# The first mixer of a two-layer trunk: one input block of the recurrent branch ahead of the queries, the other behind, and the gates as a process of their own

## The chip, the core and the metric

The kernel runs on one core of a Trainium2 chip. The metric is the device time of one execution in microseconds (us). Five engines work beside each other: TensorE (PE, with its weight loads PEld), VectorE (DVE), ScalarE (ACT), GpSimd (POOL) and SyncE (SP), which issues most of the transfers. Each engine works through its own row of instructions in order and waits at semaphores for the others.

## The reference

A trunk of two layers over 512 tokens of width 1024, all in float32, with a modulation of every sub-layer by a condition `c`. The first layer is the one that matters here:

```python
def layer_ab(...):
    sh_m, sc_m, g_m, sh_f, sc_f, g_f = adaln(c, mod_w, mod_b)       # silu(c) @ mod_w + mod_b
    h = modulate(x, norm_mix, sh_m, sc_m)                           # rmsnorm(x) * (1 + sc_m) + sh_m
    (a_gate, a_x, q, kc, vc, ks, vs, kw, vw, gts) = _split(h @ w_in, IN0_SIZES)
    y_a = rg_lru(causal_conv(a_x, conv_w, conv_b), wa, ba, wx, bx, lam) * jax.nn.gelu(a_gate)
    y_b = nsa_mixer(q, kc, vc, ks, vs, kw, vw, jax.nn.sigmoid(gts), ...)
    x = x + g_m[:, None, :] * (jnp.concatenate([y_a, y_b], axis=-1) @ w_out)
    h = modulate(x, norm_ffn, sh_f, sc_f)
    return x + g_f[:, None, :] * swiglu(h, wg, wu, wd)

def rg_lru(x, ...):                      # per channel
    r = sigmoid(x_blocks @ wa + ba);  i = sigmoid(x_blocks @ wx + bx)
    log_a = -8 * r * softplus(-lam)
    u = sqrt(-expm1(2 * log_a)) * (i * x)
    h[t] = exp(log_a)[t] * h[t-1] + u[t]
```

`nsa_mixer` has 8 query heads in 2 groups and works on blocks of 128 queries: attention to 31 compressed blocks, to the best 8 of 8 blocks of 64 keys (so to all that the mask allows) and to a window, summed with gates. The second layer is an attention with an indexer, again with a feed-forward; a last norm ends the trunk.

## The kernel before

**Matmuls in three passes.** A weight block of 1024 rows x 256 columns (1 MB) is loaded by SyncE into one of four buffers named `raw` (`load_next`, L163, and L167 for the parts of w_out). `split` rounds it on ScalarE to `whi` (L173) and takes the rest `wlo` on VectorE, or on GpSimd for the second half of some of w_out (L174). `passes` issues three matmuls for each of 8 contraction steps: rounded weight by rounded activation (L387), rounded weight by the rest (L388), rest by rounded activation (L389). `pair` does this for both 128-column halves of a block.

**Order of loads.** The list `entries` is the order in which blocks are loaded and split. In layer 0 it holds the input blocks of w_in ("win" window keys, "gts" gates, "q0" and "q1" queries, "ax0" and "ax1" the recurrent branch, "ag0" and "ag1" its gate branch), then four blocks of w_out. Behind each come some blocks of the modulation weights (`emit_mods`; the numbers per block are `MIX_MODS`), which share the four buffers. A modulation block is multiplied with `silu_c` on TensorE (`mod_rows`, L256, eight instructions) or, by other code, on GpSimd; L267 sums the rows.

**Order of work.** Generator processes yield modelled durations to a `Weaver`, which always advances the one of the lowest priority number that is ready. The first mixer has a process `backbone` (priority 5: window keys, gates, queries, recurrent branch, gate branch, output projection) and attention processes of higher rank, which start as soon as their queries are set. After that a list scheduler sets each engine's row at build time, so the rows of an engine are fixed when the program runs.

**Names.** Queries are evacuated from PSUM by ScalarE (L1009) and VectorE (L1010, `qs`). The recurrent branch: `lru1` is the convolution (ScalarE L863, then three VectorE taps L865, `xc`); `lru_gates` has two block-diagonal matmuls per 128 channels (L873, L875), two tanh on ScalarE (L878, L879) and a product (L880); `lru2` forms the recurrence's factors (ScalarE L889, L890, L897, GpSimd, VectorE L894) and scans (L902). The gate branch is evacuated at L1145. In attention a head's scores are L499, L500 and a mask matmul L510 into `b_sc`; maximum L515, exponential L518, transposes of the weights L534 (copied at L536), the weighted sum L555 into `b_o`; the compressed branch has L1083, L1086, L1111 and L548. The concatenated output is split into `yhi` and `ylo` (L1126 and L1127, L1159 and L1160) and goes through the output projection in two token halves, so its matmuls are 256 columns wide.

Of the kernel before, what the change touches and what calls it, by code (L numbers as in the profile page):

```python
# [19 lines left out]
KT = D // P  # L20
# [77 lines left out]
def trunk(ctx, tc, I, out):  # L98
    nc = tc.nc
    wv = Weaver()  # L100
# [8 lines left out]
    def bank(tag):  # L109
        return ps.tile([P, 512], F32, name="b_" + tag, tag=tag)  # L110
# [32 lines left out]
    def add_w(key, name, r0, nk, c0, ncols, cuts):  # L143
        entries.append(("w", key, name, r0, nk, c0, ncols, cuts))

    def add_mod(layer, part, j, handler):
        entries.append(("m", (layer, part, j), "l%d_mod_w" % layer, 0, KT, part * D + j * 256, 256, handler))
# [29 lines left out]
    def pump(share):  # L177

        jobs = state["jobs"]
        while jobs and state["done"] < share * state["total"]:  # L180
            state["done"] += 1
            jobs.pop(0)()
# [32 lines left out]
    def need(key, spread=False):  # L215

        idx = next(n for n, e in enumerate(entries) if e[0] in "wh" and e[1] == key)
        nxt = next((n for n in range(idx + 1, len(entries)) if entries[n][0] in "wh"), None)
        if nxt is None:
            nxt = idx + sum(e[0] == "f" for e in entries[idx + 1:idx + 3])  # L220
        pump(1.0)
        todo = list(range(state["proc"], nxt + 1))
        state["proc"] = max(state["proc"], nxt + 1)
        todo = [n for n in todo if entries[n][0] != "m"] + [n for n in todo if entries[n][0] == "m"]
        now = [n for n in todo if n <= idx or not spread]
        ms = [n for n in now if entries[n][0] == "m"]
        for i in now:
            if entries[i][0] != "m":
                process(i)
        if ms:  # L230
            wv.spawn(paced(ms), -5)
        jobs = [lambda i=i: process(i) for i in todo if i not in now]
        state["jobs"], state["done"], state["total"] = jobs, 0, len(jobs)
# [149 lines left out]
    def passes(o, w, rhi, rlo, nk, start=True, stop=True):  # L383

        hi, lo = w
        for k in range(nk):
            mm(o, hi[:, k], rhi(k), start=(start and k == 0), stop=False)  # L387
            mm(o, hi[:, k], rlo(k), start=False, stop=False)  # L388
            mm(o, lo[:, k], rhi(k), start=False, stop=(stop and k == nk - 1))  # L389
            yield k  # L390

    def pair(key, nk, ncut, rh, rl, tags, evac, flag=None):

        need(key)
        ws = [units.pop((key, n)) for n in range(ncut)]
        for n in range(ncut):
            o = bank(tags[n])
            m = ws[n][0].shape[-1]
            run = passes(o[:m], ws[n], lambda k: rh(k, 0, S), lambda k: rl(k, 0, S), nk)
            for k in range(nk):  # L400
                if flag is not None and n == 0:
                    yield ("until", flag(k))
                next(run)
                pump((n * nk + k + 1.0) / (ncut * nk))
                yield 3 * MM
            evac(n, o[:m], 0, S)
# [253 lines left out]
    def emit_mods(lst, n):  # L660
        for _ in range(n):
            if lst:
                l, p, j = lst.pop(0)
                entries.append(("m", (l, p, j), "l%d_mod_w" % l, 0, KT, p * D + j * 256, 256, "later"))
# [8 lines left out]
    add_mod(0, 0, 2, None)  # L673
    add_mod(0, 1, 3, None)
    add_mod(0, 0, 3, None)
    for nm, c0 in (("win", 2048), ("gts", 2304), ("q0", 1024), ("q1", 1280), ("ax0", 512), ("ax1", 768), ("ag0", 0),
                   ("ag1", 256)):
        if nm == "gts":
            entries.append(("h", ("in0", nm), W0, 0, KT, c0, 24, None))
        else:  # L680
            add_w(("in0", nm), W0, 0, KT, c0, 256, (P, P))
        emit_mods(dve_mods, MIX_MODS[nm])
# [162 lines left out]
    def layer0():  # L845
        mp = mix_ctx.enter_context(tc.tile_pool(name="mix0", bufs=1))
        rh = lambda k, t0, t1: hhi[:, k, t0:t1]
        rl = lambda k, t0, t1: hlo[:, k, t0:t1]
        T2 = ("mm", "mm")
# [10 lines left out]
        def lru1(ft, o):  # L860

            xc = XC[ft] = mp.tile([P, S], F32, name="xc", tag="xc", bufs=2)
            nc.scalar.activation(xc, o, AF.Identity, scale=cw[:, 12 + ft:13 + ft], bias=col["l0_conv_b"][:, ft:ft + 1])  # L863
            for s in (1, 2, 3):
                nc.vector.scalar_tensor_tensor(xc[:, s:], o[:, :S - s], cw[:, 4 * (3 - s) + ft:4 * (3 - s) + ft + 1],  # L865
                                               xc[:, s:], op0=OP.mult, op1=OP.add)
            wv.set(("xc", ft), LRU_WAIT)
# [15 lines left out]
        def lru2(n):  # L883

            fts = (2 * n, 2 * n + 1)
            yield ("wait", 1500.0)
            for ft in fts:
                AA[ft] = mp.tile([P, S], F32, name="la", tag="lx", bufs=4)
                nc.scalar.activation(AA[ft], R[ft], AF.Exp, scale=k8[:, ft:ft + 1], bias=k8[:, ft:ft + 1])  # L889
                nc.scalar.activation(R[ft], R[ft], AF.Tanh, scale=p8[:, ft:ft + 1], bias=p8[:, ft:ft + 1])  # L890
            for ft in fts:
                a2 = mp.tile([P, S], F32, name="a2", tag="xc", bufs=2)
                nc.gpsimd.tensor_tensor(a2, AA[ft], AA[ft], op=OP.mult)
                nc.vector.scalar_tensor_tensor(R[ft], a2, 1.0, R[ft], op0=OP.add, op1=OP.mult)  # L894
            yield ("wait", 4000.0)
            for ft in fts:
                nc.scalar.activation(R[ft], R[ft], AF.Sqrt, scale=0.25)  # L897
                nc.gpsimd.memset(R[ft][:, 0:1], 0.5)
                nc.gpsimd.tensor_tensor(R[ft], R[ft], IX[ft], op=OP.mult)
            yield ("wait", 2500.0)  # L900
            for ft in fts:
                nc.vector.tensor_tensor_scan(R[ft], AA[ft], R[ft], 0.0, op0=OP.mult, op1=OP.add)  # L902
                yield ("wait", 1200.0)
            wv.set(("lru", n))
# [142 lines left out]
        def kv_evac(br):  # L1047
            def f(n, o, t0, t1):
                if n == 0:
                    dup_k(Ks, br, o, mp, "kk", 2)  # L1050
                else:
                    v_rows(Vs, br, o, mp, "xc", 2)
            return f
# [111 lines left out]
        def backbone():  # L1165
            need(("in0", "win"))
            for n, ev in enumerate((cmp_evac, kv_evac(1))):
                for z in range(2):
                    for k in kv_g[2 * n + z]:
                        yield 3 * MM  # L1170
                    ev(z, kv_o[2 * n + z], 0, S)
            for y in pair(("in0", "win"), KT, 2, rh, rl, ("o", "o"), kv_evac(2)):
                yield y
            wv.set("kv2", CMP_WAIT)
            for y in gts_unit(("in0", "gts")):
                yield y
            for j in range(2):
                def qe(n, o, t0, t1, j=j):
                    sq_(4 * j + 2 * n, o)
                    wv.set(("q", 4 * j + 2 * n), 2000.0)  # L1180
                    wv.set(("q", 4 * j + 2 * n + 1), 2500.0)
                for y in pair(("in0", "q%d" % j), KT, 2, rh, rl, T2, qe):
                    yield y
            for j in range(2):
                for y in pair(("in0", "ax%d" % j), KT, 2, rh, rl, T2, lambda n, o, t0, t1, j=j: lru1(2 * j + n, o)):
                    yield y
                if j:
                    yield ("until", ("lru", 0))
                for ft in (2 * j, 2 * j + 1):
                    yield ("until", ("xc", ft))  # L1190
                    for y in lru_gates(ft):
                        yield y
                wv.spawn(lru2(j), -4)
            yield ("until", ("lru", 1))
            for j in range(2):
                for y in pair(("in0", "ag%d" % j), KT, 2, rh, rl, T2, lambda n, o, t0, t1, j=j: ag_evac(2 * j + n, o)):
                    yield y
            wv.spawn(y_a(), -6)
            for y in out_proj(0, mp):
                yield y  # L1200
            wv.set("mix0")

        wv.spawn(backbone(), 5)
        wv.run()
        mix_ctx.close()
# [411 lines left out]
```

## Time and profile before

| | |
|---|---|
| runs | 1302.85, 1303.10, 1303.66 us (median 1303.1) |
| profiled execution | 1303.04 us |
| its span | 1301.2 us |
| granted TensorE clock, mean | 0.990 |
| TensorE busy | 1257.3 us, 97% |
| VectorE busy | 774.1 us, 59% |
| ScalarE busy | 506.0 us, 39% |
| GpSimd busy | 268.4 us, 21% |
| transfers | 153.52 MB, mean 118 GB/s |

The profiled execution's time is 1.8 us above its span; that part lies around the program. Times on the trace's axis start at the span's start. The first mixer's backbone stands at 88 us (first query evacuation 89.34) to about 310; the gate branch's last evacuation is at 201.74, the first output matmul at 222.89. A line such as `PE b_mm L387 <- ACT whi L173: 1.8, 1, 1.8` reads: TensorE, at line 387 with output `b_mm`, waited for ScalarE's `whi` of line 173, 1.8 us in total, once, 1.8 at the longest.

### The profile page before, as it was taken

The page shows a single profiled execution, that of the slowest core. Times are in us where ns is not written, and L with a number is a line of the kernel's source. Part 1 is how long each engine was busy: PE and PEld are TensorE (multiplying, and loading weights), DVE is VectorE, ACT ScalarE, POOL GpSimd, SP SyncE. Part 2 cuts the span into 40 slices and gives each one's busy share as a digit, 9 for nine tenths or more (in the row PEclk, how much of TensorE's full clock was granted, in tenths as well). Part 3 has the DMA queues.
Part 4 walks back from the last instruction along what each step waited for, and adds up shares of the span by engine and source line. Part 5 has one row for each costly group of instructions (what it writes and reads, how often), then busy time and mean ns, then how long its engine had stood idle before and what let it go on. Part 6 is the DMA issues. An engine that isn't in the chain of part 4 may idle for free.

```text
span 1301.2 us, 17845 instructions
## 1 busy us (share of the span) xinstructions
PE 1257.3 (97%) x7024; PEld 1041.9 (80%) x7024; DVE 774.1 (59%) x1482; ACT 506.0 (39%) x935; POOL 268.4 (21%) x213
## 2 busy tenths in 40 slices
PE   6999998999999999999999997999999999999997
PEld 4777676789888888888898776778988888888886
DVE  6455876758656567656667699954833333333434
ACT  3444765534322222212235545774432222222323
POOL 2310142011225335344423422003000000000003
PEclk9999999999999999999999999999999999999999
DMA  9954123532544555656542523001232332233201
GB/s 325 261 167 142 62 67 98 133 96 98 162 129 162 169 178 172 194 193 195 170 131 65 130 44 86 1 2 45 86 97 97 97 98 97 97 97 97 99 16 65
DMA packets 151651, 153.52 MB, mean 118 GB/s; under 512 B 6632, under 2 KB 149136, under 8 KB 151568
## 3 DMA queue, kind: packets, MB, share of 16 engines
q1 hardware_dynamic: 150560, 151.24, 37.4%
q8 instruction: 55, 0.90, 0.3%
q10 hardware_dynamic: 656, 1.08, 0.2%
q14 instruction: 28, 0.23, 0.1%
q0 software_dynamic: 352, 0.07, 0.0%
HBM read 150.28 MB, written 2.10 MB: 117 GB/s over the span
## 4 chain that ended last, share of the span: by engine, by line
PE 84%; DVE 8%; ACT 3%; SPq 2%; DMA 2%; issue 1%; POOLq 0%; POOL 0%; ACTq 0%; DVEq 0%
PE b_mm L387 12%; PE b_mm L388 12%; PE b_mm L389 12%; PE b_sc L387 10%; PE b_sc L388 10%; PE b_sc L389 10%; PE b_o L555 2%; PE b_tp L534 2%; SPq L163 1%; PE b_sc L499 1%; DVE isc L1502 1%; PE b_sc L500 1%; DMA raw<-in_l_mod_w 1%; PE b_tp L256 1%; DVE m L1501 1%
## 5 line engine op out<-in xcount | busy, mean ns | idle before, releaser
L173 ACT ACTIVATE whi<-raw 128x1024 fp32r<-128x1024 f32 (+1 forms) x175 | 182.5, 1047 | 502.0 <-PE b_mm L388 206.4
L174 DVE TENSOR_TENSOR wlo<-raw,whi 128x1024 fp32r<-128x1024 f32 (+1 forms) x148 | 200.1, 1355 | 137.4 <-ACT whi L173 135.4
L387 PE MATMUL b_mm<-fh,whi 128*128 128x512 f32 x320 | 126.3, 395 | 0.0
L387 PE MATMUL b_sc<-fh,whi 128*128 128x512 f32 x320 | 124.7, 390 | 0.0
L388 PE MATMUL b_mm<-fl,whi 128*128 128x512 f32 x320 | 124.6, 389 | 0.0
L389 PE MATMUL b_sc<-fh,wlo 128*128 128x512 f32 x320 | 124.5, 389 | 0.0
L388 PE MATMUL b_sc<-fl,whi 128*128 128x512 f32 x320 | 124.5, 389 | 0.0
L389 PE MATMUL b_mm<-fh,wlo 128*128 128x512 f32 x320 | 124.4, 390 | 0.0
L285 POOL TENSOR_TENSOR raw<-raw,silu_c 128x1024 f32<-128x1024 f32 x28 | 59.8, 2155 | 229.8 <-DMA raw<-in_l_mod_w 133.1
L174 POOL TENSOR_TENSOR wlo<-raw,whi 128x1024 fp32r<-128x1024 f32 (+1 forms) x27 | 65.2, 2425 | 147.1 <-ACT whi L173 143.2
L1277 DVE TENSOR_TENSOR sg<-sg,b_sc 128x512 f32<-128x512 f32 (+1 forms) x48 | 30.5, 641 | 97.5 <-PE b_sc L389 97.5
L1404 POOL TENSOR_TENSOR xall<-xall,raw 128x512 f32<-128x512 f32 (+1 forms) x9 | 10.5, 1168 | 377.9 <-ACT ftmp L1403 377.9
L387 PE MATMUL b_mm<-hhi,whi 128*128 128x512 f32 x208 | 83.9, 408 | 2.2 <-DVE qs L1010 1.5
L389 PE MATMUL b_mm<-hhi,wlo 128*128 128x512 f32 x208 | 82.7, 398 | 0.0
L388 PE MATMUL b_mm<-hlo,whi 128*128 128x512 f32 x208 | 82.7, 398 | 0.0
L288 POOL TENSOR_TENSOR raw<-raw 128x1024 f32<-128x1024 f32 (+2 forms) x42 | 77.5, 1844 | 3.3
L389 PEld LDWEIGHTS b_mm<-fh,wlo 128*128 128x128 f32 x320 | 60.1, 188 | 13.0
L389 PEld LDWEIGHTS b_sc<-fh,wlo 128*128 128x128 f32 x320 | 60.1, 188 | 12.6
L387 PEld LDWEIGHTS b_sc<-fh,whi 128*128 128x128 f32 x320 | 60.1, 188 | 12.4
L388 PEld LDWEIGHTS b_sc<-fl,whi 128*128 128x128 f32 x320 | 60.1, 188 | 12.4
L388 PEld LDWEIGHTS b_mm<-fl,whi 128*128 128x128 f32 x320 | 60.1, 188 | 12.1
L387 PEld LDWEIGHTS b_mm<-fh,whi 128*128 128x128 f32 x320 | 60.1, 188 | 12.0
(380 smaller groups left out, 2971.4 us busy)
## 6 DMA issues: line engine op xcount, KB each, us to landing
raw<-in_l_mod_w SPq DMA_DIRECT2D x42, 1024.0 KB, 5.3
raw<-in_l_ffn_wg SPq DMA_DIRECT2D x22, 1024.0 KB, 5.4
raw<-in_l_ffn_wu SPq DMA_DIRECT2D x22, 1024.0 KB, 7.4
raw<-in_l_ffn_wd SPq DMA_DIRECT2D x19, 1024.0 KB, 4.9
raw<-in_l_w_in SPq DMA_DIRECT2D x16, 1024.0 KB, 5.5
rawm<-in_l_mod_w SPq DMA_DIRECT2D x6, 1024.0 KB, 11.3
raw<-in_l_w_out SPq DMA_DIRECT2D x12, 512.0 KB, 5.0
raw<-in_l_ffn_wd SPq DMA_DIRECT2D x4, 768.0 KB, 6.7
```

The costliest lines, as they stand in the source:

```text
L163: nc.sync.dma_start(v[:, :k0], I[name][r0:r0 + k0 * P, cs].rearrange("(k p) n -> p k n", p=P))
L173: nc.scalar.activation(hi, raw, AF.Copy)
L174: (eng or nc.vector).tensor_tensor(lo, raw, hi.bitcast(F32), op=OP.subtract)
L256: mm(b[32 * g:32 * g + 32, 0:256], sc_c[:, k:k + 1].to_broadcast([P, 32]), raw[:, k], start=(r == 0), stop=(r == 1), skip_group_check=True)
L285: nc.gpsimd.tensor_tensor(raw[:, k:k + 4], raw[:, k:k + 4], sc_c[:, k:k + 4][:, :, None].to_broadcast([P, 4, 256]), op=OP.mult)
L288: nc.gpsimd.tensor_tensor(raw[:, 0:n], raw[:, 0:n], raw[:, n:2 * n], op=OP.add)
L387: mm(o, hi[:, k], rhi(k), start=(start and k == 0), stop=False)
L388: mm(o, hi[:, k], rlo(k), start=False, stop=False)
L389: mm(o, lo[:, k], rhi(k), start=False, stop=(stop and k == nk - 1))
L534: nc.tensor.transpose(b[:, j * P:(j + 1) * P], pt[:, j * P:(j + 1) * P], ident)
L555: mm(o[64 * z:64 * z + 64, cs].rearrange("p (h q) -> p h q", h=nh), v[:, kb, z * 64:(z + 1) * 64], pT[z][:, :, kb * P:(kb + 1) * P], start ...
L1277: nc.vector.tensor_tensor(t, t, o, op=OP.mult)
```

## The change

The block "ax0" moves ahead of "q0" in `entries`, with the modulation blocks that follow it. `backbone` is cut into `queries(j)`, `recurrent(j)` and `gates(j)`, and its order becomes recurrent 0, queries 0, queries 1, recurrent 1. `gates(j)`, which the backbone went through itself right behind the recurrent block, is spawned as a process of priority 4, one ahead of the backbone.

```diff
-    for nm, c0 in (("win", 2048), ("gts", 2304), ("q0", 1024), ("q1", 1280), ("ax0", 512), ("ax1", 768), ("ag0", 0),
-                   ("ag1", 256)):
+    for nm, c0 in (("win", 2048), ("gts", 2304), ("ax0", 512), ("q0", 1024), ("q1", 1280), ("ax1", 768),
+                   ("ag0", 0), ("ag1", 256)):
...
-            for j in range(2):
-                def qe(n, o, t0, t1, j=j):
+            def queries(j):
+                def qe(n, o, t0, t1):
                     sq_(4 * j + 2 * n, o)
                     wv.set(("q", 4 * j + 2 * n), 2000.0)
                     wv.set(("q", 4 * j + 2 * n + 1), 2500.0)
-                for y in pair(("in0", "q%d" % j), KT, 2, rh, rl, T2, qe):
+                return pair(("in0", "q%d" % j), KT, 2, rh, rl, T2, qe)
+
+            def recurrent(j):
+                for y in pair(("in0", "ax%d" % j), KT, 2, rh, rl, T2, lambda n, o, t0, t1: lru1(2 * j + n, o)):
                     yield y
-            for j in range(2):
-                for y in pair(("in0", "ax%d" % j), KT, 2, rh, rl, T2, lambda n, o, t0, t1, j=j: lru1(2 * j + n, o)):
-                    yield y
+                wv.spawn(gates(j), 4)
+
+            def gates(j):
                 if j:
                     yield ("until", ("lru", 0))
                 for ft in (2 * j, 2 * j + 1):
...
                 wv.spawn(lru2(j), -4)
+
+            for part, j in ((recurrent, 0), (queries, 0), (queries, 1), (recurrent, 1)):
+                for y in part(j):
+                    yield y
             yield ("until", ("lru", 1))
```

The first place is VectorE's row at the start of the backbone; `qs` rows evacuate queries, `xc` rows are taps of the convolution, `mod_` rows sum modulation blocks.

```order
 L174 TENSOR_TENSOR wlo<-raw,whi 128x1024
-L1010 SCALAR_TENSOR_TENSOR qs<-b_mm,qs 64x512
+L865 SCALAR_TENSOR_TENSOR xc<-b_mm,V_91,xc 128x511
 L1074 TENSOR_SCALAR gates<-gates 128x96
-L1010 SCALAR_TENSOR_TENSOR qs<-b_mm,qs 64x512
+L865 SCALAR_TENSOR_TENSOR xc<-b_mm,V_91,xc 128x510
+L865 SCALAR_TENSOR_TENSOR xc<-b_mm,V_91,xc 128x509
 L244 TENSOR_TENSOR mod_2_899<-b_tp,V_90 128x2
 L174 TENSOR_TENSOR wlo<-raw,whi 128x1024
-L1010 SCALAR_TENSOR_TENSOR qs<-b_mm,qs 64x512
+L865 SCALAR_TENSOR_TENSOR xc<-b_mm,V_91,xc 128x511
```

Six taps take the place of the first four query evacuations, which come behind.

The second place is TensorE's row ahead of the first output matmul (`L387 ... yhi,whi`). `b_sc` rows are scores, `pr` transposes, `b_o` weighted sums. Before, the last ten rows; the modulation block whose buffer the first w_out load takes is another L256 row, nine rows above the first one shown:

```order
L256 MATMUL b_tp<-raw,silu_c 32x256 x8
L534 MATMUL b_tp<-ident,pr 128x128 x3
L267 MATMUL b_tp<-quarter,mrow 128x1 x2
L534 MATMUL b_tp<-ident,pr 128x128 x6
L499 MATMUL b_sc<-khi,qs 128x512
L500 MATMUL b_sc<-klo,qs 128x512
L510 MATMUL b_sc<-cmask,identr 128x128
L555 MATMUL b_o<-pT,vt_690 64x256 x6
L534 MATMUL b_tp<-ident,pr 128x128 x3
L387 MATMUL b_mm<-yhi,whi 128x256
```

Now, behind the head (384 columns wide) that follows the block which frees the buffer:

```order
L555 MATMUL b_o<-pT,vt_820 64x512 x4
L499 MATMUL b_sc<-khi,qs 128x384
L500 MATMUL b_sc<-klo,qs 128x384
L510 MATMUL b_sc<-cmask,identr 128x128
L267 MATMUL b_tp<-quarter,mrow 128x1 x2
L499 MATMUL b_sc<-khi,qs 128x384
L500 MATMUL b_sc<-klo,qs 128x384
L510 MATMUL b_sc<-cmask,identr 128x128
L1111 MATMUL b_tp<-ident,cpc 128x128 x2
L534 MATMUL b_tp<-ident,pr 128x128 x3
L387 MATMUL b_mm<-yhi,whi 128x256
```

The heads of 512 columns (query block 3) are gone from there, and heads of 384 columns (query block 2) stand in their place. A row counts instructions of the program; the chip runs L256, L555 and L267 as two for each.

The third place is SyncE's row at the loads of w_out, with the semaphores that each load waits for (`DMAHW` counts landed transfers, `PE`, `DVE` and `Pool` the engine's progress). Before:

```order
L163 DMA raw<-in_l_mod_w 128x8x256 [waits DMAHW5_49,PE_49]
L163 DMA raw<-in_l_w_out 128x4x256 [waits DMAHW6_49,PE_49]
L167 DMA raw<-in_l_w_out 64x4x256 x2
L163 DMA raw<-in_l_mod_w 128x8x256 [waits DMAHW7_49,PE_49]
L163 DMA raw<-in_l_w_out 128x4x256 [waits DMAHW4_49,DMAHW3_49,DMAHW5_49,DVE_49,Pool_49]
```

Now:

```order
L163 DMA raw<-in_l_mod_w 128x8x256 [waits DMAHW5_49,PE_49]
L163 DMA raw<-in_l_w_out 128x4x256 [waits DMAHW6_49,PE_49]
L167 DMA raw<-in_l_w_out 64x4x256 x2
L163 DMA raw<-in_l_mod_w 128x8x256 [waits DMAHW4_49,DMAHW3_49,DMAHW5_49,DVE_49,Pool_49]
L163 DMA raw<-in_l_w_out 128x4x256 [waits DMAHW7_49,PE_49]
```

The wait for the splits on VectorE and GpSimd has moved from the second w_out load to the modulation load in front of it, and the second w_out load waits for TensorE alone.

## The prediction

> **What bounds the kernel now.** I read the page's totals first, then the busy time by stage of the first mixer, then what TensorE waited for there, and last the queues that feed it.
>
> The totals: span; busy time of each engine; shares of the chain that ended last.
>
> ```profile
> span 1301.2 us, 17845 instructions
> PE 1257.3 (97%) x7024; PEld 1041.9 (80%) x7024; DVE 774.1 (59%) x1482; ACT 506.0 (39%) x935; POOL 268.4 (21%) x213
> PE 84%; DVE 8%; ACT 3%; SPq 2%; DMA 2%; issue 1%; POOLq 0%; POOL 0%; ACTq 0%; DVEq 0%
> ```
>
> TensorE is busy for 97% and carries 84% of the chain. The change removes no matmul, so it can act only on the 3% in which TensorE stands still and on the clock. The first mixer's stages (us; busy of PE, PEld, DVE, ACT, POOL; granted clock; DMA share; GB/s):
>
> ```profile
> 88.00:128.00 40.00, 40.00 (x232) 31.37 (x231) 20.58 (x42) 17.35 (x39) 0.00 (x0) 1.00 0.49 158
> 128.00:165.80 37.80, 36.32 (x214) 24.91 (x212) 33.02 (x82) 29.95 (x77) 5.90 (x6) 1.00 0.18 57
> 165.80:201.60 35.80, 35.76 (x186) 27.67 (x186) 25.91 (x53) 22.23 (x46) 16.63 (x15) 1.00 0.19 60
> 201.60:222.90 21.30, 17.78 (x153) 12.01 (x152) 14.58 (x38) 12.14 (x30) 3.58 (x3) 1.00 0.51 148
> 222.90:234.70 11.80, 11.74 (x85) 9.80 (x85) 9.96 (x24) 6.62 (x16) 2.38 (x1) 0.86 0.51 140
> ```
>
> Queries, recurrent and gate-branch blocks (88 to 201.6) leave 40.00+37.80+35.80 minus 40.00+36.32+35.76, that is 1.5 us of idle. The stretch from 201.6 to the first matmul of the output projection (222.9) alone leaves 21.30-17.78 = 3.5 us, and behind it stands the only low clock, 0.86. So the first mixer is decided where the output projection begins. TensorE's waits there (engine, tile, line, what it waited for; total, times, longest):
>
> ```profile
> PE b_mm L387 <- ACT whi L173: 1.8, 1, 1.8
> PE b_sc L499 <- ACT pr L518: 1.7, 4, 0.9
> PE b_mm L875 <- ACT lr L878: 0.8, 1, 0.8
> PE b_tp L534 <- DVE pT L536: 0.7, 1, 0.7
> ```
>
> The largest, in order of time with what fed it (start, duration; in brackets idle before and its releaser):
>
> ```profile
> 205.48 0.55 PE L534 MATMUL b_tp<-ident,pr 128*128 128x128 f32 x3 [0.70 <-DVE pT L536]
> 208.52 0.44 PE L499 MATMUL b_sc<-khi,qs 128*128 128x384 f32 x1 [0.88 <-ACT pr L518]
> 212.63 1.07 PE L256 MATMUL b_tp<-raw,silu_c 128*32 128x256 f32 x16
> 213.76 0.37 SPq L163 DMA_DIRECT2D raw<-in_l_w_out  x1
> 216.68 0.37 SPq L163 DMA_DIRECT2D raw<-in_l_mod_w  x1
> 221.78 1.06 ACT L173 ACTIVATE whi<-raw 128x1024 fp32r<-128x1024 f32 x1 [3.59 <-DMA raw<-in_l_w_out]
> 222.89 0.38 PE L387 MATMUL b_mm<-yhi,whi 128*128 128x256 f32 x1 [1.79 <-ACT whi L173]
> ```
>
> The modulation block at 212.63 reads one of the four weight buffers; when it ends, SyncE issues the load of the first half of w_out into that buffer (213.76), the load lands before 221.78, the rounding takes 1.06 and the first matmul starts at 222.89. From 213.70 to 222.89 are 9.2 us, TensorE had 7.4 us of other work, and 1.79 us stayed empty. The clock behind that gap:
>
> ```profile
> 224.00:229.00 5.00, 5.00 (x30) 4.92 (x30) 4.74 (x9) 1.79 (x6) 2.38 (x1) 0.66 0.20 60
> 225.00:226.00 1.00, 1.00 (x7) 1.00 (x6) 1.00 (x1) 0.66 (x3) 1.00 (x1) 0.50 0.00 0
> ```
>
> At a mean of 0.66, (1-0.66) x 5 = 1.7 us are lost there.
>
> **The change part by part.** *Instructions.* Matmuls, loads and evacuations are as many as before, so this costs 0. What remains is where work stands.
>
> *The recurrent block ahead of the queries, gates as a process of their own.* The second matmul group of a pair of gates waited once:
>
> ```profile
> 129.88 1.12 PE L875 MATMUL b_mm<-xc,bd_wx 128*128 128x512 f32 x2 [0.84 <-ACT lr L878]
> ```
>
> That wait stays in the new order, where the two groups still stand beside each other. What comes earlier is VectorE's and ScalarE's work: six taps (L865), the gates' products and the scan now stand on VectorE ahead of query evacuations (L1010). Cover: in 88 to 128 VectorE is busy for 20.58 of 40 us and ScalarE for 17.35, so the moved work fits, and the cost is 0; if the cover is gone, a query pair waits for its PSUM buffer, and the nearest row is that 0.84. Bounds -0.8 (the wait vanishes) and +0.8; I take +0.3, since both engines work in order.
>
> *Attention later against the backbone.* The first score head needs a query block, and that now comes one input block later. The first evacuations of the two query blocks show how long a block takes with what is woven into it:
>
> ```profile
> 89.34 0.58 ACT L1009 ACTIVATE qs<-b_mm 64x512 fp32r<-64x512 f32 x1
> 104.56 0.59 ACT L1009 ACTIVATE qs<-b_mm 64x512 fp32r<-64x512 f32 x1
> ```
>
> So attention is some 15.2 us late against the backbone. In the order, the last input block now ends in the score heads of query block 2 (384 columns), where before those of query block 3 had begun. Heads, transposes and products that filled 201.6 to 222.9 are there later instead. The two waits at 205.48 and 208.52 belong to a stretch whose work now stands elsewhere: -1.6 (bounds -1.6 and 0).
>
> *First output matmul.* Its load still waits for a modulation block to free the buffer. Between that block's last matmul and the first output matmul now stand three score heads, eight weighted-sum matmuls, one small modulation sum, two transposes of the compressed branch and three of attention. Their prices:
>
> ```profile
> 203.38 0.42 PE L499 MATMUL b_sc<-khi,qs 128*128 128x384 f32 x1
> 203.87 0.49 PE L534 MATMUL b_tp<-ident,pr 128*128 128x128 f32 x3
> 204.12 0.42 PE L499 MATMUL b_sc<-khi,qs 128*128 128x384 f32 x1
> 168.26 1.87 PE b_o L555 x8
> 234.35 0.22 PE b_tp L1111 x2
> 234.57 0.34 PE b_tp L267 x4
> ```
>
> A head is 203.87-203.38 = 0.49, three transposes 0.25. Work: 3 x 0.49 + 1.87 + 0.34 + 0.22 + 0.25 = 4.15 us. The load's time when nothing shares the DMA engines:
>
> ```profile
> 226.82 0.37 SPq L163 DMA_DIRECT2D raw<-in_l_w_out  x1
> 233.59 2.00 ACT L173 ACTIVATE whi<-raw 128x1024 fp32r<-128x1024 f32 x2 [0.90 <-issue]
> ```
>
> That is 6.77; shared with the modulation load of 216.68 it was 221.78-213.76 = 8.02. In the new order that next load is held (below), so I take 6.77 + 0.06 + 1.06 + 0.05 = 7.94, and idle 7.94-4.15 = 3.8 us, against 1.79: +2.0. Bounds: 0 (other heads slip in, as much idle as before) and +3.3 (8.02 in place of 6.77).
>
> *Second half of w_out.* On SyncE's queue a modulation load stands between the two halves. Before, it waited for TensorE only and was gone at 216.68. Now it waits for the splits of the first half, the GpSimd one last, and the second half is queued behind it although its own buffer is free. After the first output matmul came:
>
> ```profile
> 223.29 1.04 ACT L173 ACTIVATE whi<-raw 128x1024 fp32r<-128x1024 f32 x1
> 224.42 2.38 POOL L174 TENSOR_TENSOR wlo<-raw,whi 128x1024 fp32r<-128x1024 f32 x1 [18.34 <-ACT whi L173]
> 234.77 0.37 PE L387 MATMUL b_mm<-yhi,whi 128*128 128x256 f32 x1
> ```
>
> The GpSimd split ended 226.80-222.89 = 3.91 after it, and there the second half was issued, alone: matmul at 234.77, 11.9 after, and TensorE was busy for 11.74 of the 11.80 between. Now the chain is 3.93 + 0.43 (the modulation load's issue ahead) + 8.02 (two loads share) + 1.06 + 0.05 = 13.5. Between the two matmuls stand 24 matmuls of 256 columns, a modulation block, two heads, nine transposes, two products of the compressed branch and a modulation sum. The rows that still lack:
>
> ```profile
> 235.57 0.28 PE L388 MATMUL b_mm<-ylo,whi 128*128 128x256 f32 x1
> 235.69 0.28 PE L389 MATMUL b_mm<-yhi,wlo 128*128 128x256 f32 x1
> 230.60 1.00 PE b_tp L256 x16
> 194.11 0.27 PE b_o L548 x2
> ```
>
> 24 x 0.12 + 1.00 + 2 x 0.49 + 3 x 0.25 + 0.27 + 0.34 = 6.2; with the transposes 0.1 dearer each time, 6.4. Loss 13.5-6.4 = 7.1 us, against none. Bounds: 0 (the load isn't held after all) and 8.3 (two loads in a row at 1.2 us more).
>
> *Clock.* Before, 1.7 us behind the first gap. After, a halving behind the first matmul only stretches work that would wait anyway, and one behind the second costs 1.7: net 0 (bounds -1.7, +1.7). The trace halves the clock after a gap of 1.79 us. The Trainium skill ("TensorE: Matmul & The Clock Gate", HAM oscillation) says that gaps above about 3.4 us are what throttles; the row at 225.00 doesn't agree, since 1.79 was enough. By the page, if score heads break up the idle before the second matmul into pieces below 3.4 us, nothing is halved and the sum is 1.7 lower (1309.6); by the row it is as below.
>
> *The tail.* Attention that ran later is left when the backbone is through the output projection, with less to mix it with: from 0 to +2; I take +0.5, because the stage behind the output projection hides all but 47.50-44.30 = 3.2 us already:
>
> ```profile
> 275.50:323.00 47.50, 44.30 (x364) 43.65 (x364) 36.02 (x93) 19.76 (x35) 6.91 (x3) 1.00 0.35 111
> ```
>
> The sum: 0.3 - 1.6 + 2.0 + 7.1 + 0 + 0.5 = +8.3 us. The profiled execution took 1303.04 us, 0.06 below the median of 1303.1: 1311.3.
>
> **The rivals.** (a) *Only one wait is paid.* If the held load finds the GpSimd split done early, or its two loads share less, one of 2.0 and some 5 remains: 1303.04 + 0.3 - 1.6 + 0.5 + 3.5 to 5.8, so 1305.7 to 1308. For it: the old order hid 11.7 of 11.8 us there. Against it: the waits are fixed by the program's order.
>
> (b) *No change*: TensorE, at 97%, does the same work, and stalls only move (within 2.6 us). For it: idle of 88 to 201.6 is only 1.5 us, so the front hardly matters. Against: the queue at the output projection.
>
> (c) *Faster.* VectorE and ScalarE, at 33.02 and 29.95 of 37.80 us where the recurrent blocks stood together, are relieved by spreading these; the gates' wait (0.84), the two of attention (1.6), the first output gap (1.79) and its half clock (1.7) go: 1303.04-5.9 = 1297 at best, 1299 with half. It decides if the buffer of the first half comes free at least 7.94 us of TensorE work ahead of its matmul; I count 4.15.
>
> (d) *Larger.* Both waits, each at its upper end (+3.3, +8.3), the late attention starved of filler (+2) and a half clock more (+1.7): 1303.04+0.3-1.6+3.3+8.3+1.7+2 = 1317, so 1315 to 1317.
>
> **How the numbers follow.** Forecast (both waits, 1308 to 1315): 0.45. (a) 0.20, (b) 0.15, (c) 0.10, (d) 0.10. The likeliest is the sum, 1311.3. The range takes the forecast, (a), most of (b) and the lower part of (d): 1302.0 to 1316.5, leaving out (c), a third of (b) and a quarter of (d), 0.18. The forecast's own range is 1308 to 1315. No change means within 0.2% (2.6 us), about what a measurement of this kernel can tell. Slower: 0.45+0.20+0.10 = 0.75; same 0.15; faster 0.10.
>
> **What the profile after would show.** Right: the wait of the first output matmul for the rounding of w_out at 3 to 5 us; a second one of 5 to 8 us about 13.5 us later; SyncE's modulation load issued just when the GpSimd split ends, the w_out load right behind; slices at clock 0.5 behind both; stretches before the gate branch about as busy as now. Wrong: the second w_out load issued within 3 us of the first, a first gap below 2 us, or a query pair that waits over 1 us for its buffer. What would make the prediction wrong above all is a modulation load that isn't held, since 7.1 of 8.3 us hang on it.

## The result and the profile after

The changed kernel took 1315.97 us in the median of four runs (1315.20 to 1319.59), the kernel before 1302.97 (four runs, 1301.09 to 1303.66): ratio 1.0109, interval 1.0096 to 1.0122. So it is slower, as forecast, but by 13 to 14 us and not by 8.3; the ratio on the old median of 1303.1 gives 1317.3, above the range's upper end of 1316.5. One execution of a kernel below (late attention alone) fell into a slower state of the chip, 1410.33 us at a granted clock of 0.845, and is left out of that kernel's figure.

The profiled execution took 1316.55 us. Its page, the lines that answer to those of before:

```profile
span 1314.4 us, 17824 instructions
PE 1260.8 (96%) x7024; PEld 1044.6 (79%) x7024; DVE 772.3 (59%) x1482; ACT 504.1 (38%) x933; POOL 268.0 (20%) x213
PE 82%; DVE 9%; ACT 4%; DMA 2%; issue 1%; POOL 1%; SPq 0%; POOLq 0%; ACTq 0%; DVEq 0%
```

TensorE's share of the chain falls from 84 to 82%. To see where the time went, I cut the first mixer at two points that exist in both: the first output matmul and the norm's column sum (L356) that ends the mixer, with 240 us as a cut between. The cut at 240 is a time and not one place in the work: it lies 17.1 us behind the first output matmul before and 34.4 behind it now. Columns as in the stages of before. The kernel before, then the changed one:

```profile
85.00:222.89 137.89, 132.85 (x805) 97.46 (x803) 94.83 (x215) 81.93 (x190) 26.11 (x24) 1.00 0.32 100
222.89:240.00 17.11, 17.05 (x127) 15.06 (x128) 15.20 (x34) 10.28 (x23) 4.88 (x2) 0.90 0.52 134
240.00:308.36 68.36, 66.12 (x545) 58.92 (x543) 43.15 (x97) 28.95 (x59) 5.53 (x2) 1.00 0.30 91
```

```profile
85.00:205.56 120.56, 114.52 (x670) 84.78 (x668) 80.75 (x173) 69.07 (x158) 25.30 (x24) 1.00 0.34 105
205.56:240.00 34.44, 30.10 (x225) 24.91 (x226) 19.36 (x43) 13.86 (x35) 4.92 (x2) 0.85 0.55 153
240.00:320.73 80.73, 74.33 (x585) 64.19 (x582) 54.43 (x129) 36.01 (x77) 5.53 (x2) 1.00 0.17 53
```

The mixer ends at 320.73 instead of 308.36, 12.4 us later. Idle time of TensorE (length less busy) was 5.0, 0.1 and 2.2 us in the three stretches and is 6.0, 4.3 and 6.4. Clock loss in the middle stretch was 1.7 and is about 4.3: 2.8 and 1.5 behind the two gaps below, summed over slices of 1 us as (1 - clock) x busy. Differences: 1.0, 4.2, 4.2 and 2.6, together 12.0; another 0.4 stands ahead of 68 us. The output projection itself begins 17.3 us earlier, at 205.56, but its second token half needs attention's last heads and begins at 289.15 (276.79 before). From there to the norm the two kernels are alike, before and changed:

```profile
276.79:308.36 31.57, 30.96 (x257) 30.68 (x257) 21.36 (x46) 12.88 (x21) 5.53 (x2) 1.00 0.32 101
289.15:320.73 31.58, 30.97 (x257) 30.69 (x257) 21.37 (x46) 12.88 (x21) 5.53 (x2) 1.00 0.32 101
```

So all of the 12.4 us is lost ahead of the second token half.

Round the first two of the four blocks of w_out (the prediction calls them its halves), in order of time (start, duration, idle before and its releaser):

```profile
196.22 1.07 PE L256 MATMUL b_tp<-raw,silu_c 128*32 128x256 f32 x16
197.35 0.37 SPq L163 DMA_DIRECT2D raw<-in_l_w_out  x1
199.11 1.94 PE L555 MATMUL b_o<-pT,vt 128*64 128x512 f32 x8 [1.20 <-DVE pT L536]
204.27 0.44 PE L1111 MATMUL b_tp<-ident,cpc 128*128 128x128 f32 x2 [1.71 <-DVE cpc L1107]
205.56 0.51 PE L387 MATMUL b_mm<-yhi,whi 128*128 128x256 f32 x1 [0.53 <-ACT whi L173]
206.53 2.45 POOL L174 TENSOR_TENSOR wlo<-raw,whi 128x1024 fp32r<-128x1024 f32 x1 [6.95 <-ACT whi L173]
207.40 1.94 PE L256 MATMUL b_tp<-raw,silu_c 128*32 128x256 f32 x16 [1.12 <-ACT pT L538]
209.01 0.38 SPq L163 DMA_DIRECT2D raw<-in_l_mod_w  x1
209.49 0.53 SPq L163 DMA_DIRECT2D raw<-in_l_w_out  x1
218.53 2.00 ACT L173 ACTIVATE whi<-raw 128x1024 fp32r<-128x1024 f32 x2 [5.19 <-DMA raw<-in_l_w_out]
219.64 0.58 PE L387 MATMUL b_mm<-yhi,whi 128*128 128x256 f32 x1 [3.20 <-ACT whi L173]
```

The held load is there: the GpSimd split ends at 208.98, the modulation load is issued at 209.01, the w_out load behind it at 209.49, and the second block's first output matmul stands at 219.64, 14.1 us after the first block's (13.5 were worked out). But the hold hardly delays the w_out load. That load waits for TensorE, and what it waits for is the modulation block at 207.40, which reads its buffer until 209.34, just as the first w_out load (197.35) waited for the block that ends at 197.29. Had the modulation load not been held, the w_out load could have gone some 0.1 us earlier. What the modulation load ahead can still do is to make the transfer longer (below).

The idle time ahead of the first output matmul is there too, 3.4 us in pieces of 1.20, 1.71 and 0.53, but only the last piece was ended by the rounding of w_out. The other two are attention's own waits for VectorE, and they stand just so, 1.20 and 1.71, in the kernel with the split on VectorE (below), whose first output matmul doesn't wait for the rounding. Behind both places the clock is at one half:

```profile
209.00:210.00 1.00, 1.00 (x7) 0.73 (x4) 1.00 (x3) 0.38 (x1) 0.00 (x0) 0.50 0.00 0
221.00:222.00 1.00, 1.00 (x7) 1.00 (x6) 0.00 (x0) 1.00 (x5) 1.00 (x1) 0.50 0.00 0
```

The third stretch is new. TensorE's waits in 236 to 292 of the changed kernel, and in 236 to 279 of the one before:

```profile
PE b_sc L499 <- ACT pr L518: 2.0, 4, 0.8
PE b_mm L387 <- ACT yhi L1126: 1.3, 1, 1.3
PE b_o L555 <- DVE pT L536: 0.9, 1, 0.9
PE b_sc L387 <- ACT pr L518: 0.8, 2, 0.5
PE b_tp L534 <- DVE pT L536: 0.3, 1, 0.3
PE b_tp L534 <- DVE pr L527: 0.3, 1, 0.3
```

```profile
PE b_mm L387 <- ACT yhi L1126: 1.4, 1, 1.4
PE b_sc L499 <- ACT pr L518: 0.3, 1, 0.3
```

Eight waits more, none above 0.9 us, each for a step of one head's softmax. It reads as if the backbone had too little left to put between the last query block's heads; the experiments with late attention try this.

### The profile page after: what moved, and what is told of

It is laid out like the page before. It is cut to its first block, busy times and chain, and to the rows that moved or that the text cites. A ratio compares the mean times of both kernels' runs of the same rounds, so it can differ in the third digit from the quotient of the medians.

```text
span 1314.4 us, 17824 instructions
## 1 busy us (share of the span) xinstructions
PE 1260.8 (96%) x7024; PEld 1044.6 (79%) x7024; DVE 772.3 (59%) x1482; ACT 504.1 (38%) x933; POOL 268.0 (20%) x213
## 4 chain that ended last, share of the span: by engine, by line
PE 82%; DVE 9%; ACT 4%; DMA 2%; issue 1%; POOL 1%; SPq 0%; POOLq 0%; ACTq 0%; DVEq 0%
PE b_mm L387 12%; PE b_mm L388 11%; PE b_mm L389 11%; PE b_sc L387 10%; PE b_sc L389 10%; PE b_sc L388 10%; PE b_o L555 2%; PE b_tp L534 2%; DVE isc L1509 2%; DVE m L1508 1%; PE b_tp L256 1%; PE b_sc L499 1%; DMA raw<-in_l_w_out 1%; DMA raw<-in_l_w_in 1%; DVE qs L1010 1%
## 5 line engine op out<-in xcount | busy, mean ns | idle before, releaser
L174 DVE TENSOR_TENSOR wlo<-raw,whi 128x1024 fp32r<-128x1024 f32 (+1 forms) x148 | 196.9, 1333 | 125.1 <-ACT whi L173 119.6
L387 PE MATMUL b_mm<-fh,whi 128*128 128x512 f32 x320 | 126.3, 395 | 0.0
L387 PE MATMUL b_sc<-fh,whi 128*128 128x512 f32 x320 | 124.8, 390 | 0.0
L387 PE MATMUL b_mm<-hhi,whi 128*128 128x512 f32 x208 | 82.9, 403 | 2.3 <-DVE qs L1010 2.3
L387 PEld LDWEIGHTS b_sc<-fh,whi 128*128 128x128 f32 x320 | 60.1, 188 | 12.4
L387 PEld LDWEIGHTS b_mm<-fh,whi 128*128 128x128 f32 x320 | 60.1, 188 | 12.0
## 6 DMA issues: line engine op xcount, KB each, us to landing
rawm<-in_l_mod_w SPq DMA_DIRECT2D x6, 1024.0 KB, 11.6
```

The lines of the kernel that those rows point to most:

```text
L174: (eng or nc.vector).tensor_tensor(lo, raw, hi.bitcast(F32), op=OP.subtract)
```

## The experiments

Two theories at first. *Queue theory*, the prediction's: the time is lost to the held load and its clock. *Attention theory*: attention is a chain with its own pace; the changed order starts it later, and the second token half waits for its end. "Ahead" below is how many of attention's 64 score instructions (L499) stand ahead of the first output matmul in the program: 49 before, 38 in the changed kernel. The stretch from 240 us to the norm is shown for most kernels, since its right edge is the mixer's end (before: 308.36, after: 320.73). A load is called held when the modulation load between the first two w_out blocks waits for the GpSimd split. Each kernel was profiled once, while the runs of one kernel spread by 2 to 8 us, and the work ahead of the mixer alone shifts it by -0.4 to +0.9 us between the profiles. So differences of 1 us between two mixers, or between a mixer and a timed median, mean little.

**Order alone, gates inline.** Ahead: 39; load not held.

```diff
-                wv.spawn(gates(j), 4)
+                for y in gates(j):
+                    yield y
```

> The changed order of the blocks, but the gates in the backbone's own sequence as before. On SyncE's queue the modulation load between the two halves of w_out waits for TensorE alone again, so it is not held; attention still begins as late as in the changed kernel (39 of 64 score instructions stand ahead of the first output matmul, 38 there, 49 before). Queue theory (the time is lost to the held load and its clock): the 8.6 us lost between the two output matmuls shrink to about 3.3 (chain of 11.9 less 8.6 of work): 5 us below the changed kernel, about 1311. Attention theory (attention is a chain with a pace of its own that starts about 15 to 20 us later, and the output projection's second token half waits for its end): within 2 us of the changed kernel, 1314 to 1318.

1309.14 us, ratio 1.0046 (1.0034 to 1.0058), below both figures and nearer the queue theory's 1311.

```profile
208.97 0.37 SPq L163 DMA_DIRECT2D raw<-in_l_w_out  x1
240.00:314.05 74.05, 68.18 (x538) 59.52 (x538) 48.86 (x116) 32.55 (x68) 5.53 (x2) 1.00 0.18 58
```

The mixer's end comes 6.7 us ahead of the changed kernel's, and still 5.7 behind before's; the stretch's idle is 5.9, nearly that of the changed kernel. Both theories hold a part. But the second w_out load goes no earlier, 4.5 us behind the first output matmul (204.50) against 3.9, and its own matmul stands 15.4 us behind, at 219.88. It waits for nothing there, because more work stands between. Nor does attention keep a fixed pace: its scores run from 115.67 to 269.24, 153.6 us, where before they took 168.3 (95.42 to 263.67).

**Gates' process alone**, blocks in the old order. Ahead: 48; load not held.

```diff
-            for part, j in ((recurrent, 0), (queries, 0), (queries, 1), (recurrent, 1)):
+            for part, j in ((queries, 0), (queries, 1), (recurrent, 0), (recurrent, 1)):
```

(with `entries` in the old order)

> The gates as a process of their own, the blocks in the order of before. The modulation load is not held, 48 of 64 score instructions stand ahead of the first output matmul, but only about 4 us of TensorE work stand between the modulation block that frees the buffer and that matmul. Queue theory: a first gap of about 3.9 instead of 1.8 us, and 11.9 less 8.5 = 3.4 us lost ahead of the second half: 1303.0 + 2.1 + 3.4 - 1.7 = 1307 to 1309. Attention theory: attention starts and ends as before, 1303 within 2 us.

1307.78 us (two runs at 1302.8, five at 1307.8 to 1308.7), ratio 1.0031 (1.0016 to 1.0047), so by its median the queue theory's figure. But the profiled execution, at 1302.80, ends the mixer at 308.35, as before, with 2.6 idle behind 240; what the longer executions add was not profiled and stays open.

**Late attention alone.** The kernel before, with one number changed twice (ahead: 38).

```diff
-                    wv.set(("q", 4 * j + 2 * n), 2000.0)
-                    wv.set(("q", 4 * j + 2 * n + 1), 2500.0)
+                    wv.set(("q", 4 * j + 2 * n), 17000.0)
+                    wv.set(("q", 4 * j + 2 * n + 1), 17500.0)
```

> The kernel before, with one number changed: the flag that releases the queries to attention is set 15 us later in the planner's time, so attention stands as late against the backbone as in the changed kernel (38 of 64 score instructions ahead of the first output matmul), while the blocks, the gates and the modulation load that isn't held stay as before. Queue theory: the second output matmul has 10.2 us of work ahead in a chain of 11.9, so 1.7 lost there: 1303 to 1306. Attention theory: as late as the changed kernel, 1312 to 1318.

1310.25 us in the median of five runs, ratio 1.0060 (1.0047 to 1.0073), between the two theories and nearer the attention theory. Neither block order nor gates nor load order changed.

```profile
240.00:315.34 75.34, 69.31 (x546) 60.34 (x544) 50.12 (x119) 33.40 (x69) 5.47 (x2) 1.00 0.18 57
```

The end is 7.0 us later. Of this, 3.8 are idle behind 240 (6.0 against 2.2 before), the part which the prediction had at 0.5. Most of the rest is half clock from 206 to 217, which costs 4.7 us against 1.7 before; it follows waits of 2.22 and 1.10 us for `yhi` and `ylo` at the first output matmuls, with no load held.

**Late by 8 us** (10000 and 10500 in the same lines; ahead: 44).

> The kernel before with the queries' release to attention set 8 us later in the planner's time (44 of 64 score instructions ahead of the first output matmul; 38 with 15 us later, 49 before). If late attention is what leaves the stretch behind the first token half's projection without filler, its cost grows with the lateness: between before and the kernel with 15 us, 1304 to 1308, with some of the 4.2 us of gaps behind 240 us. If it were a fixed cost of another order: 1310.

1304.86 us, ratio 1.0024 (1.0012 to 1.0035), between before and the 15 us.

```profile
240.00:307.45 67.45, 63.55 (x514) 56.78 (x511) 43.84 (x99) 28.97 (x59) 5.53 (x2) 1.00 0.20 63
```

Idle behind 240 is 3.9, so the tail grows with the lateness. The mixer's end, at 307.45, is not later than before: the wait ahead of the first output matmul is 0.52 there instead of 1.79, and no half clock follows it (1.7 us lost before). The timed 0.24% isn't seen in this mixer.

**The changed kernel, split on VectorE** (ahead: 38; the modulation load not held).

```diff
-POOL_LO = {"in1": (0, 1), "out1": (0, 1), "out0": (1,)}
+POOL_LO = {"in1": (0, 1), "out1": (0, 1)}
```

> The changed kernel, with the second column half of w_out split on VectorE (1.36 us) instead of GpSimd (2.4 us). The modulation load is not held any more in the order that results; the second w_out load waits for VectorE's split. Attention stands as in the changed kernel (38 of 64). Queue theory: second output matmul 11 to 12 us after the first with 8.4 of work between: about 5 us below the changed kernel, 1311. Attention theory: at most 2 us below it, 1314 to 1317.

1311.17 us, ratio 1.0072 (1.0055 to 1.0088): 4.8 below the changed kernel.

```profile
208.67 0.37 SPq L163 DMA_DIRECT2D raw<-in_l_mod_w  x1
209.22 0.45 SPq L163 DMA_DIRECT2D raw<-in_l_w_out  x1
219.03 0.39 PE L387 MATMUL b_mm<-yhi,whi 128*128 128x256 f32 x1 [0.19 <-ACT whi L173]
```

The queue theory's 5 us are met, but not by its mechanism: both loads went only 0.3 us earlier than in the changed kernel, and the second block's matmul stands 14.2 us behind the first (204.83), not 11 to 12. What differs is the program's order, which has some 3 us more of TensorE work between the two, so the wait is 0.19 instead of 3.20 and no second half clock follows. The rest stays, with 6.2 idle behind 240.

**The changed kernel, one modulation block moved** (ahead: 40; not held).

```diff
-MIX_MODS = {..., 'ag0': 3, 'ag1': 2, 0: 1, ...}
+MIX_MODS = {..., 'ag0': 4, 'ag1': 1, 0: 1, ...}
```

> The changed kernel with one modulation block moved from behind the second gate-branch block to behind the first. The modulation load between the halves of w_out is not held any more, and the first half's load no longer waits for a late modulation block; attention stays late (40 of 64). If held load and late attention add up (some 7 and 6 us): about 7 us below the changed kernel, 1307 to 1310. If late attention costs nearly all: 1313 to 1317. If the queue costs nearly all: 1303 to 1306.

1308.19 us, ratio 1.0051 (1.0037 to 1.0065): 7.8 below the changed kernel, and 5.8 above before, the figures worked out for two costs that add up. The profiled execution, at 1311.51 the slowest of the five, ends its mixer at 315.86, 4.9 ahead of the changed kernel's and 7.5 behind before's. Here the second w_out load did go early, at 204.01, ahead of the first output matmul (207.38). That the costs add up isn't shown: the hold alone, next, cost less.

**Held load with early attention.** The kernel before with `'ag0': 2, 'ag1': 3` (ahead: 49).

> The kernel before with one modulation block moved from behind the first gate-branch block to behind the second. Attention stands as before (49 of 64 score instructions ahead of the first output matmul), but on SyncE's queue the modulation load between the two halves of w_out now waits for the GpSimd split, as in the changed kernel. If the held load costs what the prediction worked out: the chain of 13.5 us has 10.8 us of TensorE work ahead of the second half, and the first half's load has 4.9 instead of 7.4: some 2 to 5 us slower than before, 1305 to 1308. If only late attention costs: 1302.5 within 2 us.

1306.22 us, ratio 1.0030 (1.0018 to 1.0043): 3.8 above before, within what was worked out.

```profile
223.16 2.49 POOL L174 TENSOR_TENSOR wlo<-raw,whi 128x1024 fp32r<-128x1024 f32 x1 [8.80 <-ACT whi L173]
225.67 0.37 SPq L163 DMA_DIRECT2D raw<-in_l_mod_w  x1
227.81 1.07 PE L256 MATMUL b_tp<-raw,silu_c 128*32 128x256 f32 x16
228.94 0.37 SPq L163 DMA_DIRECT2D raw<-in_l_w_out  x1
236.99 0.39 PE L387 MATMUL b_mm<-yhi,whi 128*128 128x256 f32 x1 [1.06 <-ACT whi L173]
240.00:309.92 69.92, 67.68 (x559) 60.56 (x557) 43.38 (x97) 28.32 (x58) 5.98 (x3) 1.00 0.31 91
```

The modulation load is held to the split's end (225.65), but the w_out load goes only 3.3 us behind it, when the modulation block that reads its own buffer ends (228.88). So in this kernel too the hold isn't what delays it. At the second block's matmul 1.06 us are waited, against 3.20 in the changed kernel, and the mixer ends 1.6 later, 0.5 of which lies ahead of it; no half clock stands in it, which cost 1.7 before. In the program the work between the two matmuls was estimated at 10.8 us, against 6.4 in the changed kernel: what a late load costs hangs on the work that stands in front of its matmul.

**The modulation block behind the second w_out block** in the changed kernel (`0: 0, 1: 1`; ahead: 38).

> The changed kernel with the modulation block that stood between the first and the second block of w_out moved behind the second. The second w_out load is then the one that waits for the GpSimd split, and it no longer shares the DMA engines with a modulation load issued just ahead of it; attention stays late (38 of 64). If the held load's cost is the chain worked out (13.5 us shared, 11.9 alone, with 6 us of work in both): 1.2 to 2 us below the changed kernel, about 1314. If the order of the two loads itself were what costs (the queue, not the GpSimd split): 5 to 7 us below, 1309 to 1311.

1311.02 us, ratio 1.0069 (1.0056 to 1.0082): 5.0 below the changed kernel, the figure for the order of the two loads, and not the 1.2 to 2 of the chain.

```profile
216.16 0.39 PE L387 MATMUL b_mm<-yhi,whi 128*128 128x256 f32 x1 [2.02 <-ACT whi L173]
279.99 1.07 PE L256 MATMUL b_tp<-raw,silu_c 128*32 128x256 f32 x16 [0.31 <-ACT pT L538]
240.00:315.87 75.87, 71.47 (x566) 62.48 (x565) 51.81 (x122) 33.90 (x72) 5.53 (x2) 1.00 0.18 56
```

Two things that I had not counted: the w_out load, first in the queue (issued at 208.13, the modulation load at 209.91), was there for the rounding at 215.05, 6.9 us after, where it took 9.0 behind the modulation load (209.49 to 218.53), so that the second block's matmul stands 11.6 us behind the first (204.57) and not 14.1; and the modulation block now runs at 279.99, among the last heads, where the idle falls from 6.4 to 4.4.

**Both halves of w_out early**, in the kernel before (`'ag0': 4, 'ag1': 0, 0: 0, 1: 1, 2: 1`; ahead: 49).

> The kernel before with its modulation blocks placed so that both halves of w_out are loaded well ahead of the output projection (one block more behind the first gate-branch block, none behind the second and the first w_out block, one each behind the second and third w_out blocks); attention stands as before (49 of 64). The wait of 1.79 us ahead of the first output matmul, its half clock (1.7) and perhaps the two waits at 205.48 and 208.52 (1.6) go: 2 to 5 us faster than before, 1297.5 to 1300.5. If TensorE's idle there is not what decides but attention's own pace: 1302.5 within 1.

1305.54 us, ratio 1.0026 (1.0013 to 1.0039). The gap of 1.79 us is gone, idle behind 240 is 1.6, and the mixer ends at 308.36 as before, though it began 0.7 later. What makes the whole 0.3% slower lies behind this mixer and wasn't settled.

**The same with attention further ahead** (`'ag0': 5, 'ag1': 0, 0: 0, 1: 1`; ahead: 54).

> The kernel before with two modulation blocks more behind the first gate-branch block, none behind the second and the first w_out block and one behind the second: both halves of w_out load well ahead, and attention stands further ahead of the output projection (54 of 64 score instructions, 49 before). If first gap and late attention are what decides: the wait of 1.79 us and its half clock (1.7) go and no new gaps come behind 240 us, the first mixer's end (the norm's matmul at 308.36) comes 2 to 4 us earlier, 1299 to 1301. If, as with the early loads alone, these idle times only move: 308 to 309 and 1302 to 1306.

1300.80 us in the median of 12 runs (1296.55 to 1304.87), ratio 0.9985 (0.9973 to 0.9998): the one version that is not slower than before, just clear of no change. Its mixer ends at 309.31, no earlier, so the gain is not in the place that the theory named; in the profile, TensorE's clock in 700 to 860 us was 0.98 against 0.97 before. It is not a shown cause.

## Why the prediction was right and wrong

- *Instructions: 0.* Right: 7024 matmuls in both.
- *The front, +0.3; the two waits, -1.6; the first output matmul, +2.0.* Together +0.7, and +1.0 was measured up to that matmul. The front alone was 1.1 dearer (2.6 of idle in 85 to 185 us against 1.5), partly a query pair waiting 0.78 for VectorE at 125.28. The idle time ahead of the first output matmul came at 3.4 us against 3.8, but 2.9 of it are attention's waits for VectorE and only 0.53 the rounding's. From the block that frees the buffer (197.29) to the matmul the load's chain took 8.3 us (7.94 worked out), and TensorE's work ahead of it, attention's waits included, happened to end half a microsecond earlier. By its own sign, a first gap below 2 us, this step was wrong, and its size is in part luck.
- *The second half of w_out, +7.1.* Right in place and in its sum: the chain came at 14.1 us (13.5), idle of 1.12 and 3.20 and 2.8 of half clock between the two matmuls are 7.1, and the work at full clock is the rest, 7.0 (6.4). Wrong is that the load's "own buffer is free": a modulation block, counted there only as work between the matmuls, read it until 209.34, held up by the wait for ScalarE (1.12) and the half clock. So 7.1 us don't hang on the hold. By the prediction's own figures an unheld chain of 11.9 us against 6.4 of work would have lost 5.5. Four kernels in which no held load stands ahead of the second block are 4.8 to 7.8 us faster than the changed one (some 4 to 7 if each is taken against the runs of before in its own series), but in several ways: more work between (gates inline, split on VectorE), an earlier load (block moved forward) or a shorter one (block moved behind). How much the hold itself costs stays open; the traces show some 0.1 us of issue, and 2.1 in the length of the load where the modulation load no longer stands ahead of it.
- *Clock, net 0.* Behind the second matmul 1.5 were lost, against 1.7 before. Right; what fell behind the first is counted with the second half, as the prediction did.
- *The tail, +0.5.* This is the step that failed: +4.2 was measured (6.4 idle against 2.2), twice the upper bound of 2 that the prediction gave it. It had the place wrong, too. What is left of attention does not stand behind the output projection but ahead of its second token half, which needs the last heads, so that all of its waits move the mixer's end. I had seen that attention would be late (15 us worked out; its first scores came at 107.46 instead of 95.42) and had no price for that. The row I leaned on, 3.2 us idle in 275.5 to 323, described a stretch in which attention had already ended, and no row of before shows the last query block's heads with so little beside them. The delay of 15 us in the old order reproduces it without any of the change's other parts (6.0 idle behind 240), and 8 us gives less (3.9). With the tail at 4.2 the sum would have been +12.0, 1315.
- *Start.* 0.4 us ahead of 68 us, where TensorE's row is the same in both; not predicted.
- *Rivals.* The larger case (d), given 0.10 at 1315 to 1317, is what came, by one of the mechanisms that it listed: late attention starved of other work, at 4.2 us where (d) allowed 2, and not by both waits at their upper ends. The faster case (c) failed at its own decisive point: between the freeing block and the matmul there were 4.8 us of work where 7.94 were needed. Even the removal of that gap in the old order, which (c) counted at 1.79 and 1.7, brought at most 0.7 us to the mixer's end.
- *The clock rule.* Gaps of 1.20, 1.71 and 0.53 were followed by half clock from 206 to 212, and the gap of 3.20 by another from 220 to 222, as the 1.79 was before. The Trainium skill ("TensorE: Matmul & The Clock Gate", HAM oscillation) has gaps above about 3.4 us as what throttles. This trace doesn't agree, and the row decided rightly.

What stays open: the hold's own share; the timed differences of three kernels (gates alone, 8 us late, both halves early) whose first mixer is no longer than before's, and the gain of the last one.

## What to carry to other kernels

When a change moves work between two interleaved streams, ask for each stream when it ends, what waits for that end, and what is left to fill its gaps then. A late stream of dependent steps pays at its end, where the profile of before shows nothing because it was covered. A late load costs only what the work in front of its matmul doesn't cover: 14.1 us behind the first matmul it was waited for 3.20 us in the changed kernel, and 14.2 us behind it 0.19 with the split on VectorE. When a load is held, look also at what else it waits for: here its own buffer came free only 0.4 us after the hold ended. And order in a queue has a price: one load of 1 MB took 9.0 us behind another and 6.9 ahead of it.

## What the runs showed of the hardware

Half clock did not follow from the length of the gap alone. In the held kernel of before a single gap of 1.65 us left the clock at 1.00:

```profile
184.54 0.41 PE L1111 MATMUL b_tp<-ident,cpc 128*128 128x128 f32 x2 [1.65 <-DVE cpc L1107]
183.00:193.00 10.00, 8.46 (x47) 6.24 (x48) 8.49 (x22) 5.96 (x15) 3.68 (x4) 1.00 0.00 1
```

In the kernel with attention further ahead a shorter one, 1.55 us and alone in its stretch, was followed by 0.50:

```profile
218.91 0.48 PE L534 MATMUL b_tp<-ident,pr 128*128 128x128 f32 x1 [1.55 <-DVE mod L244]
220.00:221.00 1.00, 1.00 (x4) 0.76 (x3) 0.98 (x4) 0.72 (x3) 0.00 (x0) 0.50 1.02 344
```

Two gaps close together don't decide it either. Gaps of 1.20 and 1.71 us within 7 us came ahead of half clock in the changed kernel; in the held kernel, a gap of 1.48 and one of 0.67 four us earlier left the clock at 1.00 over the whole of 200 to 240 us:

```profile
200.00:240.00 40.00, 35.47 (x281) 27.00 (x280) 31.17 (x70) 23.30 (x53) 10.02 (x7) 1.00 0.49 132
217.16 0.55 PE L534 MATMUL b_tp<-ident,pr 128*128 128x128 f32 x3 [1.48 <-DVE pT L536]
```

In that stretch TensorE was idle for 4.5 us of 40 in several pieces. What tells these cases apart was not tried.
